# TensorE's order written out from the key projection to the last value product, in a Fourier and attention layer

## The chip, the cores and the metric

The kernel runs on one core of a Trainium2 chip. The metric is the device time of one execution in microseconds. Its engines are named as the profile names them: PE (TensorE, the matmuls), ACT (ScalarE), DVE (VectorE), POOL (GpSimd) and SP, which issues most of the DMA transfers.

## The reference

One layer of a generative model is computed for 128 context tokens and 1024 latent tokens, 1152 in all, with a width of 1024. Each layer is a normalisation with per-token-kind scale and shift, one joint projection, a Fourier mixer and a windowed attention side by side, a gated merge, and then an MLP.

```python
def merge_branches(u_f, attn_o, g, w_fo, w_ao, w_out):
    gates = jax.nn.sigmoid(g)
    g_f, g_a = gates[..., :D_MODEL], gates[..., D_MODEL:]
    m = g_f * (fourier_mix(u_f) @ w_fo) + g_a * (attn_o @ w_ao)
    return m @ w_out

def latent_layer(x, mod, k_ctx, v_ctx, cos, sin, g1, g2, w_in, sink, w_fo, w_ao, w_out, w_ff1, w_ff2):
    sh1, sc1, ga1, sh2, sc2, ga2 = mod
    h = rmsnorm(x, g1) * (1 + sc1) + sh1
    u_f, q, k, v, g = split_projection(h, w_in)
    ...
    attn_o = latent_attention(q, k, v, k_ctx, v_ctx, sink)
    x = x + ga1 * merge_branches(u_f, attn_o, g, w_fo, w_ao, w_out)
    h = rmsnorm(x, g2) * (1 + sc2) + sh2
    x = x + ga2 * channel_mixer(h, w_ff1, w_ff2)
    return x
```

The six vectors `sh1` to `ga2`, the modulation, are `silu(c) @ w_ada + b_ada`, with a weight of 1024 x 6144. Queries and keys are rotated (rotary embedding), and each block of 128 latent tokens sees three blocks of latent keys and 128 cached context keys. There are 16 query heads in four groups; a group shares one key and value head.

## The kernel before

All data is fp32. For a matmul an operand is split into a high and a low part in a shorter format: ACT casts the high part, DVE subtracts it to get the low one (`whi` and `wlo` for a weight, line 146 and line 141). One product is then three matmuls: high by high, high by low, low by high. The normalised input is held transposed in `BR` and `BT`, high and low.

The stages in the order of time are these (times of the profiled execution):

- 0 to 85 us: the normalisation, and the projection `u` of the Fourier branch.
- 85 to 182 us: the Fourier mix, four groups of channels. Products with cosine and sine matrices (`dhi`, `dlo`) alternate with casts of their results (`pqh`, line 555). Gate projections (tile `mm`, results `z` to the scratch tensor `z_d`) fill PE between them.
- 182 to 260 us: keys and values, `tok_proj_round`: round 0 for six tiles of 128 tokens, round 1 for three, in six PSUM banks. A round runs over eight slices k of the weight; in each k a tile gets three matmuls of 512 columns (lines 232 to 234), so 18 matmuls per k in round 0 and 9 in round 1. `evac_kv` splits the values, rotates the keys, stores both (`vh_d`, `kr_d`) and copies the keys of group 0 to `kd` (line 702, POOL). Then the queries of group 0, `q_pieces(0)`: six pieces of 24 matmuls with 384 columns, in two PSUM banks `mm`, rotated by DVE, stored to `q_d` and read back transposed as `qT` (line 736).
- 260 to 710 us: 36 attention units, one for each group and block of tokens. A unit has four score products (lines 755, 756), softmax, transposes of the probabilities (line 789) and value products (lines 804, 805) into one accumulator bank `o`, which `out_v` evacuates through `ot` and `at` (line 814) and stores to `att_d`. Pieces of later queries and gates stand as filler between these. For the first 34 units PE's order is the order of the code (a manual schedule); everywhere else a scheduler orders the instructions of each engine.
- 680 to 756 us: the last units, the projection of the Fourier result (`f_unit`, lines 910, 912 and 926: for each of eight blocks of 128 columns 13 matmuls of 512 columns and 13 of 130), results by ACT and DVE (`kd` and `macc`, later `fo` and `fy`, lines 914 to 917) to `part_d`; then the attention output is read back as `z` (line 1116) and split into `ER` (line 1128 and line 141).
- 756 to 980 us: the product with `w_ao`, the gated merge, the product with `w_out`. From 980 us the MLP.

The modulation vectors of the later parts are computed beside all this, without PE, in 16 blocks of ten steps (`mod_blocks`), each block 256 columns of `w_ada`. Steps 0 to 7 load 128 KB (`mraw`, line 305), let ACT scale it twice (line 309) into `macc` or, from step 1, into the only buffer `mprod`, and let POOL add it (line 311). Steps 8 and 9 are a transpose and a sum on DVE (lines 327, 328) into `red`. A fold, `mod_fold`, is one small matmul `mm <- red, quads` (line 274) with four DVE sums behind it; it is issued at step 5 of the following block. `mod_step(n)` issues n steps. Before the change 40 steps lie in the Fourier mix, 72 in the attention units, 8 behind them and 40 in the MLP. From the tail on the scalings and sums run on DVE alone (lines 316, 318).

Of the kernel before, what the change touches and what calls it, by code (L numbers as in the profile page):

```python
# [57 lines left out]
def backbone_kernel(  # L58
# [284 lines left out]
    with ExitStack() as sf:  # L343
# [175 lines left out]
        for gi in range(4):  # L519
# [71 lines left out]
            mod_step(MOD_F)  # L591

    with ExitStack() as s1x:
# [4 lines left out]
        identr = p1.tile([P, P], F32R, name="identr")  # L598
        nc.scalar.copy(identr, ident)
# [66 lines left out]

        with ExitStack() as skv:
# [59 lines left out]
            tok_proj_round(ROUNDS[0], OFF_KV, bankk, evac_kv)  # L727
            tok_proj_round(ROUNDS[1], OFF_KV, bankk, evac_kv)
# [67 lines left out]
        def out_v(u, b):  # L796
            k0, nb = KWIN[u["i"]]
            if b == 0:
                u["o"] = q1.tile([P, 512], F32, tag="o", name=nm("o"), bufs=1)
            po = u["o"]  # L800
            ph, pl = u["p"].pop(b)
            kb = {"c": 9, "x": 8}.get(KT_ORDER[k0 + b], KT_ORDER[k0 + b])
            vst = u["v"][:, kb].rearrange("p a d -> p (a d)")
            nc.tensor.matmul(po, vst, ph, start=(b == 0), stop=False)
            nc.tensor.matmul(po, vst, pl, start=False, stop=(b == nb - 1))
            if b < nb - 1:
                return
            ot = p1.tile([P, 2, P], F32, tag="ot", name=nm("ot"), bufs=1)
            at = p1.tile([P, 2, P], F32, tag="at", name=nm("at"), bufs=1)
            pv = po.rearrange("p (r e t) -> p e r t", r=2, e=2)  # L810
            for e in range(2):
                top, bot = slice(64 * e, 64 * e + 64), slice(64 - 64 * e, 128 - 64 * e)
                nc.scalar.copy(ot[top], pv[bot, e])
                nc.vector.tensor_tensor(at[top], pv[top, e], ot[top], ALU.add)
# [26 lines left out]

        fexw = (slot(8)[:, 0:FC][0:96], slot(9)[:, 0:D][0:96])

        def load_fx():
            wfo.append(load_wfo(0))
            for i in range(4):
                raw = raw_w([P, FC])
                nc.sync.dma_start(raw, f_d[i])
                hi, lo = (slot(2 * i + e)[:, 0:FC] for e in range(2))
                nc.scalar.copy(hi, raw)  # L850
                sub(nc.vector, lo, raw, hi)
                fx.append((hi, lo))
            raw = raw_w([P, FC])
            nc.gpsimd.memset(raw, 0.0)
# [10 lines left out]
            nc.scalar.copy(wex, raw[0:96])  # L865
            sub(nc.vector, wex[64:68], raw[64:68], wex[64:68])
# [17 lines left out]
        funits = [(m, j) for m in range(KC) for j in range(2)]  # L884
        fbank = [mmt]
        fbuf = []

        def f_mm(ps, ops, ex, c, r, n):
            wh, wl = wfo[0]
# [4 lines left out]
            if ex is not None:  # L894
                seq.append((ex, fexw[0]))
            for i, (w, x) in enumerate(seq):
                yield ps, w, x[:, r], i == 0, i == len(seq) - 1

        def f_unit(n):
            for _ in range(min(n, len(funits))):  # L900
                m, j = funits.pop(0)
                if m % 2 == 0 and j == 0 and m:
                    wfo[0] = load_wfo(m)
                c = slice((m % 2) * P, (m % 2) * P + P)
                wex = fexw[1][:, m * P : (m + 1) * P]
                if j == 0:
                    lat = slice(0, 512)
                    psy, psx = fbank[0](), fbank[0]()
                    for ps, w, x, a, z in f_mm(psy, (2, 3), None, c, lat, 512):
                        nc.tensor.matmul(ps, w, x, start=a, stop=z)  # L910
                    for ps, w, x, a, z in f_mm(psx, (0, 1), wex, c, lat, 512):
                        nc.tensor.matmul(ps, w, x, start=a, stop=z)
                    y, o = fbuf[0]()
                    nc.scalar.copy(y, psy)
                    nc.vector.tensor_tensor(o[:, 0:512], psx, y, ALU.subtract)
                    nc.vector.tensor_tensor(o[:, 1023:512:-1], psx[:, 1:512], y[:, 1:512], ALU.add)
                    nc.scalar.copy(o[:, 0:1], psx[:, 0:1])
                    nc.sync.dma_start(part_d[m][:, 0:512], o[:, 0:512])
                    nc.sync.dma_start(part_d[m][:, 513:1024], o[:, 513:1024])
                    continue  # L920
                ps = fbank[0]()
                ctx_ = list(f_mm(ps, (0, 1), wex, c, slice(512, 642), 130))
                cty_ = list(f_mm(ps, (2, 3), None, c, slice(512, 640), 128))
                for _, w, x, _, _ in ctx_[:1] + cty_ + ctx_[1:]:
                    n = x.shape[1]
                    nc.tensor.matmul(ps[:, 0:n], w, x, start=x is ctx_[0][2], stop=x is ctx_[-1][2])
                z = zpool[0].tile([P, CH], F32, tag="z", name=nm("z"), bufs=ZB[0])
                nc.scalar.copy(z[:, 0:130], ps[:, 0:130])
                nc.sync.dma_start(part_d[m][:, 1024:1152], z[:, 0:128])
                nc.sync.dma_start(part_d[m][:, 512:513], z[:, 128:129])  # L930

        def fbuf_p1():
            y = p1.tile([P, 2, MB], F32, tag="macc", name=nm("macc"), bufs=1)
            o = p1.tile([P, 10, 2, HD], F32, tag="kd", name=nm("kd"), bufs=1)
            return y.rearrange("p a n -> p (a n)"), o.rearrange("p a b d -> p (a b d)")

        fbuf.append(fbuf_p1)
# [3 lines left out]
        man = ExitStack()  # L941
        man.enter_context(tc.manual_schedule(engines={mybir.EngineType.PE}))
        for piece in q_pieces(0):
            for _ in piece:
                pass
        for q in range(3):
            put_k(kv[0][0], q)

        blocks_, pieces_ = [], []
        gate_left = gate_ids[48 - len(gates) :]  # L950
        share = -(-len(gate_left) // NG)
        gw = {}
        for g in range(NG):
            if g + 1 < NG:
                ws = q_weights(g + 1)
                for n, pc in enumerate(q_pieces(g + 1, ws)):
                    pieces_.append((pc, len(blocks_) + n % 2, g + 1 if n == 5 else None))
                blocks_ += ws
            for _ in range(min(share, len(gate_left))):
                m, j = gate_left.pop(0)  # L960
                if m not in gw:
                    gw[m] = (OFF_GF + m * P, {}), len(blocks_)
                    blocks_.append(gw[m][0])
                pieces_.append((gate_piece(m, j, gw[m][0]), gw[m][1], None))
        NSUB = KC * len(pieces_)
        qdone = {0}
        done = [0]

        def fill_steps():
            for pc, b, q in pieces_:  # L970
                for w in blocks_[: b + 2]:
                    fetch(w)
                for _ in pc:
                    yield
                if q is not None:
                    qdone.add(q)
                yield
# [13 lines left out]
        NMAN = len(units) - 2  # L991
# [3 lines left out]
        def begin(s):  # L995
            g, i = units[s]
            for g1, i1 in units[s : s + 4 : 3] if i % 3 == 0 else ():
                if (g1, i1 // 3) not in qts:
                    assert g1 in qdone, (s, g1)
# [3 lines left out]
        def next_keys(g, i):  # L1003
            if i == 0 and g:
# [25 lines left out]
        base, pending, late = 0.0, None, []  # L1030
        for s in range(NMAN):
            u = begin(s)
            order = unit_order(s, u, pending, late)
            share = NSUB * weight(s) / wsum
# [9 lines left out]
            pending = u  # L1044
        fill_to(NSUB)
        for _ in steps_:
            pass
        man.close()
        for s in range(NMAN, len(units)):
            u = begin(s)  # L1050
            for h in range(4):
                score_head(u, h)
                if late:
                    out_v(*late.pop(0))
            nb = KWIN[pending["i"]][1]
            for b in range(nb):
                out_t(pending, b)
                out_v(pending, b)
            pending = u
            if s == NMAN:  # L1060
                load_fx()
            f_unit(NF)
        mod_step(len(msteps) - MOD_B)
        mod_fold()
        f_unit(NF2)
        for b in range(KWIN[8][1]):
            out_t(pending, b)
            out_v(pending, b)
# [1022 lines left out]
```

## Time and profile before

| | us |
|---|---|
| runs | 1690.02, 1695.48, 1694.44 |
| median | 1694.44 |
| the profiled execution | 1695.82 |
| its span | 1694.0 |
| PE busy | 1624.9 (96%) |
| DVE busy | 1134.8 (67%) |
| ACT busy | 912.3 (54%) |
| POOL busy | 290.4 (17%) |

The span runs from the first to the last instruction of the profile; the 1.8 us beside it lie around the program. A busy time of 96% is a mean over the stages: it is near the whole in most of them and lower in the tail. A PE that is busy need not be at its full pace, since its clock is granted in parts; the mean clock over the span is 0.984 of full speed. In a view of waits, "PE o L804 <- DVE at L814: 10.5, 3, 4.1" reads: the matmul of line 804 into `o` waited three times for the DVE instruction of line 814 that writes `at`, 10.5 us in all and 4.1 us at the longest.

### The profile page before, as it was taken

The numbers are of one execution on the slowest core, as the hardware profiler recorded it, in microseconds if no ns is written. First come the engines' busy times: TensorE is split into PE (matmuls) and PEld (weight loads), VectorE is DVE, ScalarE is ACT, GpSimd is POOL, SyncE is SP. The second block draws the span as 40 slices with busy tenths as digits, with TensorE's granted clock in tenths as the row PEclk, the third lists the DMA queues.
The fourth block names the chain that finished last, engine by engine and source line by source line (L and its number), as shares of the span: only waits on it lengthen the run. The fifth ranks groups of instructions, "written<-read, shape, count | busy, mean of one in ns | idle before, by whom it ended". The sixth has DMA issues, their size and how long they took to land.

```text
span 1694.0 us, 24957 instructions
## 1 busy us (share of the span) xinstructions
PE 1624.9 (96%) x8421; PEld 1430.3 (84%) x8421; DVE 1134.8 (67%) x2147; ACT 912.3 (54%) x1775; POOL 290.4 (17%) x382
## 2 busy tenths in 40 slices
PE   6999998999999999789999899999999999999998
PEld 5789888899999999679988788888888888888886
DVE  7665266767767766657657876777776488776764
ACT  7766225676676766536436664444444353444542
POOL 1055013344344344500001500000000200000000
PEclk9999999999999999879999999999999999999999
DMA  8353487535453432468546434455446996666751
GB/s 300 125 171 105 164 212 162 130 102 131 122 137 101 130 95 77 135 192 290 162 172 202 153 109 149 163 168 168 159 152 156 307 389 196 194 195 191 248 162 63
DMA packets 221136, 285.41 MB, mean 168 GB/s; under 512 B 30968, under 2 KB 148664, under 8 KB 220880
## 3 DMA queue, kind: packets, MB, share of 16 engines
q1 hardware_dynamic: 212752, 273.85, 51.3%
q0 software_dynamic: 8256, 9.96, 2.6%
q8 instruction: 66, 1.08, 0.3%
q14 instruction: 62, 0.51, 0.1%
HBM read 205.87 MB, written 77.88 MB: 167 GB/s over the span
## 4 chain that ended last, share of the span: by engine, by line
PE 49%; DVE 2%; issue 2%; ACT 1%; DMA 1%; POOL 0%; SPq 0%; POOLq 0%; ACTq 0%; DVEq 0%
PE x L1817 6%; PE x L1816 6%; PE x L1818 6%; PE x L1420 6%; PE x L1422 6%; PE x L1421 6%; PE x L196 2%; PE x L194 2%; PE x L195 2%; PE mm L1467 1%; PE mm L1466 1%; PE mm L1465 1%; PE mm L1817 1%; PE mm L1816 1%; PE mm L1818 1%
## 5 line engine op out<-in xcount | busy, mean ns | idle before, releaser
L141 DVE TENSOR_TENSOR wlo<-wraw,whi 128x1024 fp32r<-128x1024 f32 x109 | 138.9, 1277 | 77.4 <-ACT whi L146 76.9
L146 ACT CAST whi<-wraw 128x1024 fp32r<-128x1024 f32 x107 | 111.8, 1049 | 91.5 <-PE x L1253 17.8
L767 ACT ACTIVATE pt<-pt,mx 128x513 f32<-128x513 f32 (+2 forms) x144 | 95.9, 666 | 78.5 <-DVE mx L757 73.5
L195 PE MATMUL mm<-BR,whi 128*128 128x384 f32 x408 | 138.0, 338 | 0.0
L779 POOL TENSOR_SCALAR pt<-pt,mx 128x512 f32<-128x512 f32 (+2 forms) x144 | 94.0, 665 | 237.1 <-DVE mx L777 230.3
L1817 PE MATMUL x<-BR 128*128 128x512 f32 (+1 forms) x348 | 132.9, 382 | 0.0
L1818 PE MATMUL x<-BR 128*128 128x512 f32 (+1 forms) x348 | 132.3, 382 | 0.0
L311 POOL TENSOR_TENSOR macc<-macc,mprod 128x512 f32<-128x512 f32 x84 | 113.5, 1352 | 108.3 <-ACT mprod L309 97.3
L194 PE MATMUL mm<-BR,whi 128*128 128x384 f32 x360 | 128.9, 358 | 2.7 <-DVE qt L638 1.9
L1816 PE MATMUL x<-BR 128*128 128x512 f32 (+1 forms) x348 | 131.4, 382 | 0.0
L757 DVE CUSTOM_DVE_ANT_0 pt<-s,mask,nsink 128x512 f32<-128x512 f32 (+2 forms) x144 | 96.1, 671 | 42.5 <-PE s L756 40.4
L196 PE MATMUL mm<-BR,wlo 128*128 128x384 f32 x360 | 122.1, 339 | 0.0
L1789 ACT CAST BR<-aa 128x512 fp32r<-128x512 f32 x80 | 49.7, 621 | 104.3 <-PE x L1817 46.4
L141 DVE TENSOR_TENSOR pl<-ptp,ph 128x512 fp32r<-128x512 f32 x124 | 83.0, 686 | 28.9 <-ACT ph L792 28.3
L309 ACT ACTIVATE mprod<-mraw,siluc 128x256 f32<-128x256 f32 x168 | 76.8, 505 | 32.1 <-POOL macc L311 31.8
L1420 PE MATMUL x<-BR,whi 128*128 128x512 f32 (+2 forms) x204 | 79.9, 391 | 4.1 <-ACT ZR L1444 2.8
L195 PEld LDWEIGHTS mm<-BR,whi 128*128 128x128 f32 x408 | 77.8, 191 | 6.3
L1421 PE MATMUL x<-BR,whi 128*128 128x512 f32 (+2 forms) x204 | 78.1, 383 | 0.0
L1422 PE MATMUL x<-BR,wlo 128*128 128x512 f32 (+2 forms) x204 | 78.0, 383 | 0.0
L792 ACT CAST ph<-ptp 128x512 fp32r<-128x512 f32 x124 | 69.9, 583 | 14.1 <-PE ptp L789 13.0
L194 PE MATMUL mm<-BT,whi 128*128 128x384 f32 x216 | 76.9, 356 | 0.0
L141 DVE TENSOR_TENSOR BR<-aa,BR 128x512 fp32r<-128x512 f32 x80 | 55.0, 687 | 32.2 <-ACT BR L1789 31.6
(448 smaller groups left out, 4750.7 us busy)
## 6 DMA issues: line engine op xcount, KB each, us to landing
aa<-hr_d SPq DMA_DIRECT2D x108, 256.0 KB
ab<-in_w_ff_dram SPq DMA_DIRECT2D x108, 256.0 KB
hr_d<-ZR SPq DMA_DIRECT2D x104, 256.0 KB
wraw<-in_w_in_dram SPq DMA_DIRECT2D x41, 512.0 KB
wraw<-in_w_ff_dram SPq DMA_DIRECT2D x34, 512.0 KB
mraw<-in_w_ada_dram SPq DMA_DIRECT2D x96, 128.0 KB
wraw<-in_w_out_dram SPq DMA_DIRECT2D x24, 512.0 KB
z_d<-z SPq DMA_DIRECT2D x48, 192.0 KB
```

Of the source, the lines that this page charges most:

```text
L141: eng.tensor_tensor(dst, raw, hi.bitcast(F32), ALU.subtract)
L146: nc.scalar.copy(hi, raw)
L194: nc.tensor.matmul(out, ah, bh, start=start, stop=False)
L195: nc.tensor.matmul(out, ah, bl, start=False, stop=False)
L196: return nc.tensor.matmul(out, al, bh, start=False, stop=stop).ins
L311: nc.gpsimd.tensor_tensor(acc, acc, pr_, ALU.add)
L1420: nc.tensor.matmul(po, wh, xh, start=(k == 0 and not cont), stop=False, skip_group_check=cont)
L1421: nc.tensor.matmul(po, wh, xl, start=False, stop=False, skip_group_check=cont)
L1422: nc.tensor.matmul(po, wl, xh, start=False, stop=(k == 3), skip_group_check=cont)
L1816: nc.tensor.matmul(ps, xh, bh, start=start, stop=False, skip_group_check=cont)
L1817: nc.tensor.matmul(ps, xh, bl, start=False, stop=False, skip_group_check=cont)
L1818: nc.tensor.matmul(ps, xl, bh, start=False, stop=stop, skip_group_check=cont)
```

## The change

The manual schedule of PE begins ahead of key round 0 and lasts to the last value product. Its order is now: round 0, the six query pieces of group 0, round 1, the first key transposes, twelve filler steps, the next key transposes, four filler steps, all 36 units.

The modulation steps leave the Fourier mix. Fifty stand in the key rounds, issued through `before=`: four for each k in round 0, two for each k in round 1 (four at the last). `tok_proj_round`, which itself is unchanged, issues those of two k ahead: with `ahead = 2` the steps of k = 0, 1 and 2 come before the matmuls of k = 0. The attention units keep 60, ten go to the ao product, 40 to the MLP.

The Fourier projection is written as pieces. Three (`FATT`) are filler in the last two units, five follow the last value product, in the six banks of the next stage. Two of its output buffers alternate, and the buffer `at` is doubled. The weight `wex` is spread over two slots, and the copy `identr` goes.

```diff
-MOD_B = 40
-MOD_F = 10
+MOD_B = 50
 MOD_LATE = 40
-NF = 4
-NF2 = 2
+FATT = 3
...
             filler(FILL_F, anchor)
-            mod_step(MOD_F)
...
-            tok_proj_round(ROUNDS[0], OFF_KV, bankk, evac_kv)
-            tok_proj_round(ROUNDS[1], OFF_KV, bankk, evac_kv)
+            man.enter_context(tc.manual_schedule(engines={mybir.EngineType.PE}))
+            tok_proj_round(ROUNDS[0], OFF_KV, bankk, evac_kv, before=lambda k: mod_step(4))
+            for piece in q_pieces(0):
+                for _ in piece:
+                    pass
+            tok_proj_round(ROUNDS[1], OFF_KV, bankk, evac_kv, before=lambda k: mod_step(2 if k < 7 else 4))
...
-            at = p1.tile([P, 2, P], F32, tag="at", name=nm("at"), bufs=1)
+            at = p1.tile([P, 2, P], F32, tag="at", name=nm("at"), bufs=2)
...
+        def f_piece(m):
+            if m % 2 == 0 and m + 2 < KC:
+                wfo.append(load_wfo(m + 2))
+            out = []
+            for ops, ex in (((2, 3), False), ((0, 1), True)):
+                ps = fbank[0]()
+                seq = f_mm(m, ops, ex)
+                for i, (w, x) in enumerate(seq):
+                    nc.tensor.matmul(ps, w, x[:, 0:512], start=i == 0, stop=i == len(seq) - 1)
+                    if i % 2 == 1 and i < len(seq) - 1:
+                        yield
+                out.append(ps)
...
+            nc.vector.tensor_tensor(o[:, 0:512], psx, y, ALU.subtract)
+            nc.vector.tensor_tensor(o[:, 1023:512:-1], psx[:, 1:512], y[:, 1:512], ALU.add)
...
-        NSUB = KC * len(pieces_)
+        NSUB = KC * len(pieces_) + FSUB * FATT
+        FX_AT = len(pieces_) - 2
...
+                if n == FX_AT:
+                    load_fx()
...
+            for _ in range(FATT):
+                for _ in f_piece(fleft.pop(0)):
+                    yield
+                yield
...
-        NMAN = len(units) - 2
+        NMAN = len(units)
...
+        put_k(kv[0][0], 0)
+        fill_to(12)
+        put_k(kv[0][0], 1)
+        fill_to(16)
...
+        for v in late:
+            out_v(*v)
+            fill_to(base + 1)
+        out_t(pending, 0)
         fill_to(NSUB)
         for _ in steps_:
             pass
+        out_v(pending, 0)
         man.close()
-        for s in range(NMAN, len(units)):
-            u = begin(s)
...
-            f_unit(NF)
         mod_step(len(msteps) - MOD_B)
         mod_fold()
-        f_unit(NF2)
```

PE at the start of round 0, before the change. The rows are the last gate filler of the Fourier mix, a fold whose steps lay in the Fourier mix, and then the first tile of round 0 (`x_1872`).

```order
L195 MATMUL mm_1744<-BR,whi_1712 128x384
L196 MATMUL mm_1744<-BT,wlo_1713 128x384
L274 MATMUL mm_1801<-red_1617,quads 128x16
L232 MATMUL x_1872<-whi_1868,BR 128x512
L233 MATMUL x_1872<-wlo_1869,BR 128x512
L234 MATMUL x_1872<-whi_1868,BR 128x512
```

PE after the change, at the end of k = 0 of round 0: the last tile of k = 0 (`x_1723`), the first fold, and the first tile of k = 1 (`x_1703`).

```order
L230 MATMUL x_1723<-whi_1699,BR 128x512
L231 MATMUL x_1723<-wlo_1700,BR 128x512
L232 MATMUL x_1723<-whi_1699,BR 128x512
L272 MATMUL mm_1745<-red_1679,quads 128x16
L230 MATMUL x_1703<-whi_1699,BR 128x512
L231 MATMUL x_1703<-wlo_1700,BR 128x512
L232 MATMUL x_1703<-whi_1699,BR 128x512
```

The fold that stood ahead of round 0 belonged to steps of the stage before; now the first block of the steps starts at round 0 and its fold stands behind 18 matmuls. The second stands behind 54 more, the third behind the query pieces, the fourth behind 36 matmuls of round 1.

ACT in the Fourier mix, before, around the first cast of `pqh`. The names are the scalings (`mprod`), the weight casts (`whi`) and the gate results (`z`).

```order
L309 ACTIVATE mprod_1380<-mraw_1378,siluc 128x256 x2
L146 CAST whi_1335<-wraw_1333 128x1024
L480 COPY z_1001<-mm_976 128x384
L309 ACTIVATE mprod_1386<-mraw_1384,siluc 128x256 x2
L146 CAST whi_1712<-wraw_1710 128x1024
L555 CAST pqh_1066<-x_1036 128x512
L309 ACTIVATE mprod_1392<-mraw_1390,siluc 128x256 x2
L555 CAST pqh_1066<-x_1037 128x256
```

ACT at the same place after the change:

```order
L478 COPY z_973<-mm_948 128x384
L144 CAST whi_1538<-wraw_1536 128x1024
L478 COPY z_1001<-mm_976 128x384
L553 CAST pqh_1066<-x_1036 128x512
L553 CAST pqh_1066<-x_1037 128x256
L531 CAST sth_1175<-st_1165 128x1152
```

The scalings are gone from between the casts; the weight cast stands one gate result earlier.

PE in the last unit after the change. The rows are a Fourier piece (`mm_7683`, line 926), scores of the last unit (`s`), and value products of the unit before it (`o_7666`). Before the change the Fourier products of lines 910 and 912 followed the scores of unit 34 in one run.

```order
L926 MATMUL mm_7683<-BR,whi_7335 128x512 x2
L755 MATMUL s_7689<-kth,qT_6925 128x128
L756 MATMUL s_7689<-ktl,qT_6925 128x128
L804 MATMUL o_7666<-ph_7641,vg_5606 128x512
L805 MATMUL o_7666<-pl_7642,vg_5606 128x512
L926 MATMUL mm_7683<-BR,wlo_7336 128x512
L926 MATMUL mm_7683<-BR,whi_7335 128x512
L755 MATMUL s_7698<-kth,qT_6925 128x128
L756 MATMUL s_7698<-ktl,qT_6925 128x128
L926 MATMUL mm_7683<-BR,whi_7335 128x512
```

Scores, value products and pieces alternate by ones and twos.

More of the change, by code (lines that the diff above doesn't have):

```diff
@@ L840, in backbone_kernel, with __getitem__ @@
         fx, wfo = [], []
-        fexw = (slot(8)[:, 0:FC][0:96], slot(9)[:, 0:D][0:96])
+        class Wex:
+            def __getitem__(self, idx):
+                o = idx[1].start
+                return slot(9 + o // 512)[:, o % 512 : o % 512 + idx[1].stop - o][0:96]
+        fexw = (slot(8)[:, 0:FC][0:96], Wex())
         def load_fx():
@@ L864, in load_fx @@
                 nc.sync.dma_start(raw[32 * k : 32 * k + 4], w_fo.rearrange("(g c) n -> g c n", g=4)[:, 64])
-            nc.scalar.copy(wex, raw[0:96])
-            sub(nc.vector, wex[64:68], raw[64:68], wex[64:68])
+            for o in range(0, D, 512):
+                r = slice(o, o + 512)
+                nc.scalar.copy(wex[:, r], raw[0:96, r])
+                sub(nc.vector, wex[:, r][64:68], raw[64:68, r], wex[:, r][64:68])
         def load_wfo(m):
@@ L882, in load_wfo, with fbuf_p1, f_mm @@
             return split(xy, [P, 4, 256])
-        funits = [(m, j) for m in range(KC) for j in range(2)]
         fbank = [mmt]
         fbuf = []
-        def f_mm(ps, ops, ex, c, r, n):
-            wh, wl = wfo[0]
+        fturn = [0]
+        def fbuf_p1():
+            fturn[0] += 1
+            if fturn[0] % 2:
+                y = p1.tile([P, 2, MB], F32, tag="macc", name=nm("macc"), bufs=1)
+                o = p1.tile([P, 10, 2, HD], F32, tag="kd", name=nm("kd"), bufs=1)
+                return y.rearrange("p a n -> p (a n)"), o.rearrange("p a b d -> p (a b d)")
+            y = p1.tile([P, 2, MB], F32, tag="mprod", name=nm("mprod"), bufs=1)
+            o = p1.tile([P, 2, 516], F32, tag="pt", name=nm("pt"), bufs=4)
+            return y.rearrange("p a n -> p (a n)"), o.rearrange("p a n -> p (a n)")
+        fbuf.append(fbuf_p1)
+        def f_mm(m, ops, ex):
+            wh, wl = wfo[m // 2]
+            c = slice((m % 2) * P, (m % 2) * P + P)
             seq = []
@@ L893, in f_mm @@
                 seq += [(wh[:, i, c], xh), (wh[:, i, c], xl), (wl[:, i, c], xh)]
-            if ex is not None:
-                seq.append((ex, fexw[0]))
-            for i, (w, x) in enumerate(seq):
-                yield ps, w, x[:, r], i == 0, i == len(seq) - 1
-        def f_unit(n):
[L900 to L937, printed above, removed]
+            if ex:
+                seq.append((fexw[1][:, m * P : (m + 1) * P], fexw[0]))
+            return seq
+        def f_piece(m):
[10 more added lines that the diff above has]
+                out.append(ps)
+                if not ex:
+                    y, o = fbuf[0]()
+                    nc.scalar.copy(y, ps)
+                    yield
+            psx = out[1]
+            nc.vector.tensor_tensor(o[:, 0:512], psx, y, ALU.subtract)
+            nc.vector.tensor_tensor(o[:, 1023:512:-1], psx[:, 1:512], y[:, 1:512], ALU.add)
+            nc.scalar.copy(o[:, 0:1], psx[:, 0:1])
+            nc.sync.dma_start(part_d[m][:, 0:512], o[:, 0:512])
+            nc.sync.dma_start(part_d[m][:, 513:1024], o[:, 513:1024])
+            yield
+            ps = fbank[0]()
+            ctx_ = [(w, x[:, 512:642]) for w, x in f_mm(m, (0, 1), True)]
+            cty_ = [(w, x[:, 512:640]) for w, x in f_mm(m, (2, 3), False)]
+            seq = ctx_[:1] + cty_ + ctx_[1:]
+            for i, (w, x) in enumerate(seq):
+                n = x.shape[1]
+                nc.tensor.matmul(ps[:, 0:n], w, x, start=i == 0, stop=i == len(seq) - 1)
+                if i % 5 == 4:
+                    yield
+            z = zpool[0].tile([P, CH], F32, tag="z", name=nm("z"), bufs=ZB[0])
+            nc.scalar.copy(z[:, 0:130], ps[:, 0:130])
+            nc.sync.dma_start(part_d[m][:, 1024:1152], z[:, 0:128])
+            nc.sync.dma_start(part_d[m][:, 512:513], z[:, 128:129])
@@ L939, in backbone_kernel @@
+        FSUB = 9
+        fleft = list(range(KC))
+        def f_unit(n):
+            for _ in range(min(n, len(fleft))):
+                for _ in f_piece(fleft.pop(0)):
+                    pass
         units = [(g, i) for g in range(NG) for i in range(NTT)]
         kv = {0: load_kv(0, kd0)}
[L941 to L947, printed above, removed]
+        for tag, n in (("s", 2), ("o", 1)):
+            for _ in range(n):
+                q1.tile([P, 512], F32, tag=tag, name=nm(tag), bufs=n)
@@ L949, in backbone_kernel, with add_gate @@
         blocks_, pieces_ = [], []
         gate_left = gate_ids[48 - len(gates) :]
+        gate_left[-4:] = gate_left[-3:] + gate_left[-4:-3]
         share = -(-len(gate_left) // NG)
         gw = {}
+        def add_gate():
+            m, j = gate_left.pop(0)
+            if m not in gw:
+                gw[m] = (OFF_GF + m * P, {}), len(blocks_)
+                blocks_.append(gw[m][0])
+            pieces_.append((gate_piece(m, j, gw[m][0]), gw[m][1], None))
         for g in range(NG):
+            if g == 0:
+                add_gate()
+                add_gate()
@@ L976, in fill_steps @@
                     qdone.add(q)
+                yield
+            for _ in range(FATT):
+                for _ in f_piece(fleft.pop(0)):
+                    yield
                 yield
@@ L1003, in next_keys @@
         def next_keys(g, i):
-            if i == 0 and g:
+            if i == 0:
                 put_k(kv[g][0], 2)
@@ L1028, in unit_order @@
             return out
-        base, pending, late = 0.0, None, []
+        put_k(kv[0][0], 0)
+        fill_to(12)
+        put_k(kv[0][0], 1)
+        fill_to(16)
+        base, pending, late = 16.0, None, []
+        NSPR = NSUB - 16 - 6
         for s in range(NMAN):
@@ L1033, in backbone_kernel @@
             order = unit_order(s, u, pending, late)
-            share = NSUB * weight(s) / wsum
+            share = NSPR * weight(s) / wsum
             spots, seen = order.count(None), 0
```

31 lines of the change are left out of this document (6 added, 25 removed).

## The prediction, made before the changed kernel ran

> **What bounds the kernel now.** I read the busy time by stage first, then what TensorE (PE) waited for, then the clock, and last the rows around each wait. Busy time of each engine in three stretches of the span: Fourier mix, key/value rounds, tail.
>
> ```profile
> 85.00:182.00 97.00, 92.88 (x504) 85.89 (x503) 54.33 (x96) 58.97 (x120) 45.78 (x36) 0.96 0.43 135
> 182.00:260.00 78.00, 76.03 (x376) 66.97 (x374) 33.51 (x65) 20.68 (x36) 6.42 (x16) 1.00 0.77 204
> 680.00:756.00 76.00, 57.04 (x278) 47.54 (x277) 42.36 (x89) 34.55 (x85) 20.22 (x28) 0.80 0.50 156
> ```
>
> The columns are stretch, length, busy us of PE, its weight loads, DVE, ACT and POOL, then the granted clock, the DMA share and GB/s. PE sets the end everywhere; the change leaves its work as it is, so the time can move only by PE's idle time and its slow clock. The tail stands out: 76.00 − 57.04 = 19.0 us idle, at a clock of 0.80. What PE waited for, over the span:
>
> ```profile
> PE o L804 <- DVE at L814: 10.5, 3, 4.1
> PE s L756 <- DVE ktl L141: 5.0, 1, 5.0
> PE x L910 <- DVE at L814: 3.8, 1, 3.8
> PE x L194 <- ACT pqh L555: 3.5, 1, 3.5
> PE mm L194 <- DVE qt L638: 1.9, 1, 1.9
> ```
>
> The first and third belong mostly to the tail. Seven stretches of the same view, cut by the granted clock (third figure from the right), show what such waits cost behind them:
>
> ```profile
> 127.95:134.70 6.75, 6.16 (x20) 5.08 (x19) 4.54 (x13) 2.29 (x6) 3.83 (x3) 0.50 0.21 68
> 241.00:243.00 2.00, 1.30 (x7) 1.31 (x8) 2.00 (x6) 1.09 (x3) 0.29 (x1) 1.00 1.08 359
> 264.50:271.20 6.70, 5.63 (x18) 5.63 (x19) 5.01 (x13) 3.19 (x7) 1.14 (x2) 0.50 1.22 277
> 701.40:715.00 13.60, 6.26 (x15) 4.10 (x14) 6.42 (x11) 6.34 (x14) 8.59 (x7) 0.50 0.39 112
> 728.70:735.50 6.80, 5.65 (x14) 4.47 (x14) 2.07 (x13) 0.58 (x1) 0.00 (x0) 0.50 0.45 125
> 739.00:745.60 6.60, 5.55 (x13) 3.87 (x13) 2.15 (x5) 1.69 (x5) 0.00 (x0) 0.50 0.90 273
> 752.60:755.80 3.20, 3.20 (x12) 3.20 (x11) 3.20 (x8) 2.26 (x6) 0.00 (x0) 0.50 0.98 319
> ```
>
> One more row of PE, the only wait at L804 that lies outside the tail:
>
> ```profile
> 310.31 0.48 PE L804 MATMUL o<-ph,vg 128*128 128x512 f32 x1 [2.86 <-DVE at L814]
> ```
>
> After waits of 3.5 and 5.0 us PE ran at half clock for 6.7 us; after the 1.9 us one it did not. Work done at half clock would have taken half its time. So the losses are: Fourier stage 3.5 + 6.16/2 = **6.6 us**; KV rounds and first units 1.9 + 5.0 + 5.63/2 + 2.9 = **12.6 us**; tail 19.0 + (6.26 + 5.65 + 5.55 + 3.20)/2 = **29.3 us**. These are all that the change can win.
>
> **The change, term by term.** The sum is made against the profiled execution, 1695.82 us (span 1694.0), 1.4 us over the median 1694.44 of the runs.
>
> *Fourier stage.* Forty modulation steps leave it. In the trace the cast `pqh` that PE waited for stood on ACT behind such a step, which waited for POOL, and behind a weight cast that waited for its load:
>
> ```profile
> 117.66 0.91 ACT L309 ACTIVATE mprod<-mraw,siluc 128x256 f32<-128x256 f32 x2 [0.74 <-POOL macc L311]
> 120.61 1.05 ACT L146 CAST whi<-wraw 128x1024 fp32r<-128x1024 f32 x1 [2.03 <-DMA wraw<-in_w_in_dram]
> 121.57 0.61 ACT L555 CAST pqh<-x 128x512 fp32r<-128x512 f32 x1
> ```
>
> Without the steps' scalings and loads it comes earlier. Bounds 2 to 6.6 us; I take **−6**, nearest to the whole since the wait and its half clock hang together.
>
> *KV rounds.* Fifty steps now stand here, and with PE's order written out, each block's fold (the small matmul `mm <- red`, L274 of before, L272 now) is a place at which PE stops until ACT, POOL and DVE have done the block's steps. The pace of a step, from seven POOL adds of one block (first and last):
>
> ```profile
> 156.40 1.29 POOL L311 TENSOR_TENSOR macc<-macc,mprod 128x512 f32<-128x512 f32 x1 [3.04 <-DVE pql L141]
> 171.00 1.30 POOL L311 TENSOR_TENSOR macc<-macc,mprod 128x512 f32<-128x512 f32 x1 [1.09 <-ACT mprod L309]
> 714.38 0.43 DVE L327 STREAM_TRANSPOSE mtr<-macc 128x256 f32<-128x256 f32 x1
> 715.78 0.42 DVE L328 TENSOR_REDUCE red<-mtr 128x8 f32<-128x256 f32 x1
> ```
>
> Six steps in 14.6 us are 2.4 us each, a chain through one `mprod` buffer: 0.9 (step 0) + 7 × 2.4 + 1.8 (four DVE instructions, 714.38 to 716.20) = 19.5 us for a block, and 18.3 for the next, whose first scalings go ahead. When it starts:
>
> ```profile
> 182.16 0.47 PE L232 MATMUL x<-whi,BR 128*128 128x512 f32 x1
> 185.49 0.33 SPq L601 DMA_DIRECT2D mask<-in_mask_dram  x1
> 188.90 2.06 SPq L305 DMA_DIRECT2D mraw<-in_w_ada_dram x3
> 196.55 0.91 ACT L309 ACTIVATE macc<-mraw,siluc 128x256 f32<-128x256 f32 x2 [0.32 <-DMA mraw<-in_w_ada_dram]
> ```
>
> The rounds began at 182.16; the weight loads stood behind mask, rotary tables and caches and ACT began at +14.4. The key rotary table and the caches are now loaded earlier, so I take +12 (from +6, about where the loads were issued, to +14). Queued behind a fold on PE are all later matmuls of the rounds, and behind the `mraw` loads on SP the later weight loads; ACT, POOL and DVE go on with the steps meanwhile. Fold 0 stands behind 18 matmuls and is ready at +31.5; fold 1 behind 72 matmuls and ready at 12 + 19.5 + 18.3 = +49.8. PE's own pace, from two rows 11 matmuls apart:
>
> ```profile
> 228.89 0.39 PE L234 MATMUL x<-whi,BT 128*128 128x512 f32 x1
> 231.39 0.39 PE L234 MATMUL x<-whi,BT 128*128 128x512 f32 x1
> ```
>
> 0.2275 us each: PE would be at fold 1 at 72 × 0.2275 = +16.4. So **33.4 us** are lost by then (27.4 to 35.4); the slow clock after fold 0 costs nothing beside it, since PE is early at fold 1 anyway. Folds 2 and 3 are covered: q(0)'s 144 matmuls (25 us) and half of round 1 lie between (a 384-column product at 384/512 of 0.2275 us).
>
> Behind fold 1: half clock again, 3 us by the row at 127.95. Then q(0)'s products need DVE, which has the six key tiles of round 0 to rotate first. In the trace ACT's first and last V casts of that round, and the read-back of q, stood at:
>
> ```profile
> 211.72 0.37 ACT L695 CAST qhl<-x 128x256 fp32r<-128x256 f32 x1 [3.71 <-PE x L234]
> 223.29 0.37 ACT L695 CAST qhl<-x 128x256 fp32r<-128x256 f32 x1 [4.70 <-DMA vh_d<-qhl]
> 245.64 1.85 SPq L736 DMA_DIRECT2D qT<-q_d  x4
> ```
>
> The six casts span 12 us, and DVE's rotations of their keys stand ahead of q's; the first two q pieces (48 matmuls, two banks) are only 8.2 us of PE: 0 to 8 us, I take 3. The q read-back is issued behind the last key store, 245.64 − 231.39 = 14 us after the rounds' last matmul; before, q's own matmuls covered that, now only key transposes and 48 gate matmuls, some 9 us, stand ahead of the first scores: 0 to 9 us, I take 5, the bare difference of the two. Sum 33.4 + 3 + 3 + 5 = 44.4, and the 12.6 of before go (`ktl`'s transposes come earlier, `at` has two buffers, the wait for q is counted anew): **+32** (+18 to +43).
>
> *Tail.* Three Fourier pieces now lie between the last scores and value products, the accumulator's evacuation has a second buffer, and five pieces follow on six banks. The waits for `at` go, with the half clock behind them. What is late next: the attention output's split (24 pairs, DVE) before the ao products, with ten modulation steps now among it.
>
> ```profile
> 752.17 3.44 DVE L141 TENSOR_TENSOR ER<-z,ER 128x384 fp32r<-128x384 f32 x7
> L318 DVE SCALAR_TENSOR_TENSOR ZR<-ZR,siluc 128x256 f32<-128x256 f32 x56 | 24.6, 476 | 1.1 <-DMA ZR<-in_w_ada_dram 1.0
> 755.53 0.68 DVE L915 TENSOR_TENSOR fo<-x,fy 128x512 f32<-128x512 f32 x1
> 726.20 0.27 PE L926 MATMUL mm<-BR,whi 128*128 128x130 f32 x1
> 726.31 0.27 PE L926 MATMUL mm<-BR,wlo 128*128 128x130 f32 x1
> ```
>
> 24 × 0.49 + 16 × 0.476 + 1.8 + 5 × 1.4 = 28 us on DVE (the splits, sixteen modulation products, their transposes, two `fo` sums for each of five pieces), against about 5 × (13 × 0.2275 + 13 × 0.11) = 22 us of PE's Fourier work (the 130-column products start 0.11 us apart): 3 to 8 us of wait, 1.7 to 3 of half clock, and 1 to 4 at the last values. About 10 us remain (5 to 16): **−19** (−13 to −24).
>
> The new second output buffer, the weights in two slots and the missing `identr` copy (0.3 us on ACT) hide behind PE and cost nothing; in the units PE's losses stay.
>
> Sum: −6 + 32 − 19 = **+7**: 1702.8, say 1702 us.
>
> **Rivals.**
>
> *The stall is shorter* (faster, 0.24). If the weight loads land as soon as they are issued (+6), nothing waits for q, and the tail runs with 5 us of loss, it is −7 + 18 − 24 = −13: 1683 us. For it: fewer loads queue ahead than before. Against: ACT's first scaling in the trace still waited for its load. It decides below a KV loss of about +20.
>
> *Balance* (within 0.3%, 0.22). Start at +9, half of the small waits: 30.4 + 3 + 3 + 2 − 12.6 = +26; with −6 and −19 this is +1: 1697 us.
>
> *The tail's clock stays low* (slower, 0.14). Two of its half-clock stretches began behind short waits:
>
> ```profile
> 728.12 0.62 PE L274 MATMUL mm<-red,quads 128*128 128x16 f32 x4 [0.64 <-ACT kd L917]
> 729.89 1.19 PE L910 MATMUL mm<-BR,whi 128*128 128x512 f32 x2 [1.15 <-DVE mods L278]
> 738.72 1.10 PE L910 MATMUL x<-BR,whi 128*128 128x512 f32 x2 [1.63 <-ACT fy L914]
> ```
>
> So 1.2 to 1.6 us among small matmuls were enough, and five pieces still follow one another over a few banks. Keeping the last three stretches costs (5.65 + 5.55 + 3.20)/2 = 7.2 us of the gain: 1709, at most 1710 us. [...]
>
> *All the new waits at their upper ends* (slower, 0.06): 35.4 + 3 + 8 + 9 − 12.6 = +43, with −6 and −19: 1714 us.
>
> That the folds do not bind would be the change not doing what it says; the order of PE's instructions shows them ahead of the matmuls, so it has no chance of its own.
>
> **How the numbers follow.** The forecast, 1702 (own range 1699.5 to 1707), has 0.34. A measurement of this kernel can tell about 0.3% (5 us) from no change. Faster by more: 0.24; within: 0.22; slower by more: 0.34 + 0.14 + 0.06 = 0.54. Signs differ, so the range runs from 1684 to 1717.
>
> **What would show it.** In the profile after: PE idle some 27 us before the first fold and 3 to 6 us before the second, released by DVE `red`, at half clock between; no wait for `pqh`; the tail's idle time halved, with no wait for `at` between the last units and the Fourier pieces, and a wait for the split of `z` before the ao products. I am wrong if the folds wait less than 25 us in all, or if the tail keeps over 20 us of loss.

## The result: 1720.7 us, slower by 1.6%

| | before | after |
|---|---|---|
| median of the runs, us | 1694.96 (4 runs) | 1720.71 (4 runs, 1719.39 to 1725.81) |
| ratio after to before, 95% interval | | 1.0163 [1.0133, 1.0192] |
| span of the profiled execution, us | 1694.0 | 1717.6 |

The change costs 26 us by the medians and 23.6 us by the two profiled spans. One of the five executions of e9 below took 5721.68 us; its ratio is taken from the other four. Busy time by stage in the profile after, in the columns of the prediction's first fence: Fourier mix, key rounds up to the first scores, attention units, tail up to the ao products.

```profile
85.00:174.00 89.00, 88.55 (x496) 82.37 (x496) 40.38 (x73) 33.91 (x58) 8.36 (x8) 1.00 0.35 110
174.00:318.00 144.00, 95.49 (x443) 84.02 (x442) 56.32 (x112) 61.40 (x123) 53.09 (x51) 0.82 0.61 154
318.00:700.00 382.00, 371.69 (x2155) 346.42 (x2155) 263.85 (x644) 256.19 (x596) 154.88 (x240) 1.00 0.41 115
700.00:785.00 85.00, 78.89 (x454) 70.09 (x454) 64.25 (x136) 48.19 (x114) 19.08 (x35) 0.98 0.59 181
```

PE's idle time is 0.5, 48.5, 10.3 and 6.1 us. To these belong the stretches at half clock, from the same view:

```profile
205.50:211.90 6.40, 6.36 (x16) 5.11 (x17) 0.63 (x4) 2.29 (x6) 3.63 (x3) 0.50 0.25 67
222.30:229.00 6.70, 4.37 (x14) 3.50 (x15) 2.78 (x8) 2.96 (x8) 2.56 (x2) 0.75 0.47 139
300.00:307.50 7.50, 4.92 (x17) 4.95 (x18) 1.12 (x2) 2.04 (x5) 2.60 (x4) 0.50 0.65 199
427.00:430.40 3.40, 3.40 (x13) 3.01 (x12) 1.03 (x3) 1.32 (x3) 1.13 (x2) 0.51 0.43 91
751.40:754.70 3.30, 3.30 (x10) 2.55 (x9) 0.00 (x0) 0.83 (x2) 0.00 (x0) 0.50 0.55 144
```

Half of the busy time there is counted as lost, as in the prediction: 3.2, 1.7 (the half clock is the second half of that stretch), 2.5, 1.7 and 1.7 us. That is a little much: at half clock products of 512 columns started 0.43 us apart (206.99 to 211.25 us), at full clock 0.2275 us, so 47% is lost by the rows. By stage, loss (idle time and half clock) before and after, in us:

| stage | before | after | difference | predicted |
|---|---|---|---|---|
| Fourier mix | 6.6 | 0.5 | −6 | −6 |
| key rounds to first units | 12.6 | 55.9 | +43 | +32 |
| attention units | 3.7 | 12.0 | +8 | 0 |
| tail | 29.3 | 7.8 | −21.5 | −19 |
| sum | | | +23.5 | +7 |

What PE waited for in the profile after:

```profile
PE mm L272 <- DVE red L326: 30.1, 2, 26.8
PE ptp L835 <- ACT rb L711: 16.4, 1, 16.4
PE o L804 <- DVE at L814: 9.2, 6, 2.3
...
PE x L926 <- DVE at L814: 2.2, 1, 2.2
...
PE x L192 <- ACT pqh L553: 0.4, 1, 0.4
```

The first row is the two folds, 26.8 and 3.3 us. The second is far above the 5 us that the prediction had ahead of the first scores: one wait of 16.4 us in front of the first key transposes, for the instruction that copies the context tile's values out (`rb`). Three rows of PE show all three, with the idle time at the end:

```profile
205.54 0.61 PE L272 MATMUL mm<-red,quads 128*128 128x16 f32 x2 [26.85 <-DVE red L326]
224.63 0.37 PE L272 MATMUL mm<-red,quads 128*128 128x16 f32 x2 [3.29 <-DVE red L326]
302.58 1.09 PE L835 MATMUL ptp<-ident,kd 128*128 128x128 f32 x4 [16.38 <-ACT rb L711]
```

`rb` and the transposes share no data: `rb` reads the bank of the last key tile, and the transposes write a bank of the next PSUM pool (`q1`), which lies on the same six banks. Of `kd` the transposes need tiles 0 to 2 and the cache alone. The profile puts the wait of their weight load down to the last copy into `kd`, which ended 0.1 us ahead of `rb`; e1 below tells the two apart. Why `rb` was so late, on ACT and on SP's queue:

```profile
289.52 1.04 ACT L144 CAST whi<-wraw 128x1024 fp32r<-128x1024 f32 x1 [7.57 <-DMA wraw<-in_w_in_dram]
...
291.74 0.35 ACT L691 CAST qhl<-x 128x256 fp32r<-128x256 f32 x1
...
297.14 1.04 ACT L144 CAST whi<-wraw 128x1024 fp32r<-128x1024 f32 x1 [3.77 <-DMA wraw<-in_w_in_dram]
300.08 0.37 ACT L691 CAST qhl<-x 128x256 fp32r<-128x256 f32 x1 [1.90 <-DMA vh_d<-qhl]
...
302.11 0.37 ACT L711 COPY rb<-x 128x256 f32<-128x256 f32 x1
```

```profile
282.50 0.91 SPq L153 DMA_DIRECT2D wraw<-in_w_in_dram  x1
283.50 8.70 SPq L303 DMA_DIRECT2D mraw<-in_w_ada_dram  x2
292.30 0.38 SPq L153 DMA_DIRECT2D wraw<-in_w_in_dram  x1
...
305.82 0.34 SPq L736 DMA_DIRECT2D qT<-q_d  x1
```

Round 1's last matmul began at 285.8. The first cast of its evacuation, `qhl`, stood on ACT behind a weight cast that waited 7.6 us for its load. The next load stood on SP behind `mraw` loads, which took 8.7 us to get out, and held up a second weight cast. The third `qhl` then waited another 1.9 us, for the store of the first to free its buffer, so that store ended last. The read-back of q, `qT`, followed at 305.8.

### The profile page after: what moved, and what is told of

Same layout as the page of the kernel before. It is cut to its first block, busy times and chain, and to the rows that moved or that the text cites. A ratio compares the mean times of both kernels' runs of the same rounds, so it can differ in the third digit from the quotient of the medians.

```text
span 1717.6 us, 24946 instructions
## 1 busy us (share of the span) xinstructions
PE 1621.3 (94%) x8421; PEld 1426.9 (83%) x8421; DVE 1133.9 (66%) x2164; ACT 909.4 (53%) x1759; POOL 279.1 (16%) x375
## 4 chain that ended last, share of the span: by engine, by line
PE 70%; DVE 5%; DMA 3%; ACT 3%; issue 2%; POOL 1%; SPq 1%; DVEq 0%; ACTq 0%; POOLq 0%
PE x L1845 6%; PE x L1843 6%; PE x L1844 6%; PE x L1447 6%; PE x L1449 6%; PE x L1448 6%; PE mm L192 4%; PE mm L194 4%; PE mm L193 4%; PE ptp L789 2%; PE x L194 2%; PE x L193 2%; PE x L192 2%; PE s L756 2%; PE o L805 2%
## 5 line engine op out<-in xcount | busy, mean ns | idle before, releaser
L309 POOL TENSOR_TENSOR macc<-macc,mprod 128x512 f32<-128x512 f32 x77 | 102.1, 1326 | 42.9 <-ACT mprod L307 32.8
L307 ACT ACTIVATE mprod<-mraw,siluc 128x256 f32<-128x256 f32 x154 | 70.2, 502 | 46.8 <-POOL macc L309 45.8
L1844 PEld LDWEIGHTS x<-BR 128*128 128x128 f32 x348 | 65.4, 188 | 12.9
```

The lines of the kernel that those rows point to most:

```text
L309: nc.gpsimd.tensor_tensor(acc, acc, pr_, ALU.add)
L1844: nc.tensor.matmul(ps, xh, bl, start=False, stop=False, skip_group_check=cont)
```

## The experiments

Each run has its median and its ratio to the kernel before, taken on the same chip. Theory A: the place of the folds in PE's written order costs. Theory B, its rival: the steps' load on the other engines does. Theories C and D concern the 16.4 us, E and F the tail.

**e1_folds_held.** The folds wait until the first units:

```diff
+    hold = [False]
+    spare = []
...
-        while fold:
+        while fold and not hold[0]:
...
+            hold[0] = True
             tok_proj_round(ROUNDS[0], OFF_KV, bankk, evac_kv, before=lambda k: mod_step(4))
...
+            hold[0] = False
```

> The changed kernel with its fifty modulation steps where they are, but the five folds held back until the first attention units (their sums kept in spare tiles). Theory A (it is the place of the folds in PE's written order that costs): the 30.1 us of waiting at L272 and the half clock behind them, 37 us in all by the profile, go; five folds in a row cost some 3 us; 1684 to 1690 us. Theory B (it is the steps' load on ACT, POOL and DVE that costs, wherever the folds stand): the wait only moves to the weight casts and to q's and the keys' evacuation; 1705 us or more.

1696.2 us, ratio 1.0004 [0.9992, 1.0016]: 24.5 us less than the changed kernel, between the two. Round 1's last matmul began at 252.8 instead of 285.8, 33 us earlier, as theory A has it, and the first scores at 278.0 instead of 315.3. Behind them some 13 us came back: among these, the five folds in a row cost 4.8 us of waits and left PE at half clock from 305.1 to 312.0. In front of the first scores two waits remain, for `rb` and for `qT`; the middle row is a wait in the rounds:

```profile
PE ptp L844 <- ACT rb L716: 9.9, 1, 9.9
...
PE mm L192 <- DVE qt L638: 3.5, 2, 3.2
PE s L764 <- DMA qT<-q_d: 3.5, 1, 3.5
```

The longest wait for q's evacuation is 3.2 us, where the changed kernel had one of 1.0 us in the rounds. Theory A carries 33 us; theory B is wrong for the rounds. Three rows show which wait the transposes have:

```profile
262.56 0.37 ACT L716 COPY rb<-x 128x256 f32<-128x256 f32 x1
263.03 1.09 PE L844 MATMUL ptp<-ident,kd 128*128 128x128 f32 x4 [9.87 <-ACT rb L716]
263.31 0.29 POOL L703 COPY kd<-qr 128x128 f32<-128x128 f32 x1
```

The transposes began 0.1 us behind the end of `rb` and ahead of the last copy into `kd`: they wait for the bank's reader, not for `kd`.

**e2_steps_back.** The steps return to the Fourier mix:

```diff
             filler(FILL_F, anchor)
+            mod_step(10)
...
-            tok_proj_round(ROUNDS[0], OFF_KV, bankk, evac_kv, before=lambda k: mod_step(4))
+            tok_proj_round(ROUNDS[0], OFF_KV, bankk, evac_kv)
...
-            tok_proj_round(ROUNDS[1], OFF_KV, bankk, evac_kv, before=lambda k: mod_step(2 if k < 7 else 4))
+            tok_proj_round(ROUNDS[1], OFF_KV, bankk, evac_kv)
```

> The changed kernel with no modulation steps in the key rounds and ten behind each group of the Fourier mix, as before the change. Theory A and theory B both: 37 us of fold waits and half clock go, 7 us of the Fourier mix (the wait for pqh) come back. Theory C (the 16.4 us in front of the first key transposes are the evacuation of round 1 with nothing ahead of it, made longer by steps and their loads): that wait falls to 10 to 12 us but stays; 1683 to 1690 us. If the wait were made by the steps alone, it would go: about 1674 us.

1683.3 us, ratio 0.9942 [0.9922, 0.9961], in the range: faster than before. Its waits:

```profile
PE ptp L836 <- ACT rb L712: 5.6, 1, 5.6
PE x L192 <- ACT pqh L553: 3.3, 1, 3.3
```

The wait for `pqh` is back with the steps, as the prediction's Fourier term has it. The wait for `rb` does not go, but at 5.6 us it is half of what was expected. Round 1's first `qhl` now begins 0.9 us ahead of the round's last matmul; in the changed kernel it began 5.9 us behind it.

**e3_gates_first.** The sixteen fillers first:

```diff
+        fill_to(16)
         put_k(kv[0][0], 0)
-        fill_to(12)
         put_k(kv[0][0], 1)
-        fill_to(16)
```

> The changed kernel with all sixteen filler steps ahead of the first key transposes instead of twelve between and four behind them: the same matmuls in another order. Theory C (the transposes' banks come free only when round 1 is evacuated, and 8.4 us of matmuls that need none of these banks stand behind them): the wait falls from 16.4 to about 8 us, 1710 to 1714 us. If the gate matmuls, too, wait for that evacuation: 1718 us or more.

1721.9 us, ratio 1.0158 [1.0139, 1.0177]: no gain, though the wait fell to 5.7 us. PE's rows:

```profile
302.88 0.45 PE L835 MATMUL ptp<-ident,kd 128*128 128x128 f32 x1 [5.73 <-ACT rb L711]
...
316.69 0.66 PE L755 MATMUL s<-kth,qT 128*128 128x384 f32 x1 [11.87 <-DMA qT<-q_d]
```

The first scores come at 316.7 as against 315.3. They wait for the read-back of q, which SP issues from 305.9 on and which lands some 10 us later. So theory C is half right: the fillers do cover the wait for the banks, but behind it runs a longer path, from round 1's last matmul through the evacuation, its last store and q's read-back to the first scores. It took 29.5 us with the steps in the changed kernel and 28.3 in e3, 25 in e1 and 20 in e2; the order of the sixteen fillers moves only where PE waits for it.

**e6_round0_only.** Round 1 is called without `before`, so that its eighteen steps fall to the units and six behind them.

> The changed kernel without the eighteen steps in round 1 (six of them then stand at the end of the units, the others within them). Theory D (the evacuation of round 1 is late since ACT stands in a weight cast that waits for its load, and the load stood on SP behind mraw loads without a free buffer): the wait at the first key transposes falls from 16.4 to about 10 us and the first two fold waits stay; 1712 to 1716 us. If the steps have no part in it: 1719 us or more.

1727.4 us, ratio 1.019 [1.017, 1.0211]: slower. The path became shorter, 21.5 instead of 29.5 us: the waits at its end are 5.5 and 4.4 us, and the first scores come at 306.6, 8.7 us earlier than in the changed kernel. So the steps of round 1 made it longer; whether by their loads on SP, as theory D has it, or by their work on ACT, the run does not tell. The loss is in the tail:

```profile
PE mm L947 <- ACT macc L932: 11.7, 1, 11.7
...
PE ptp L835 <- ACT rb L711: 5.5, 1, 5.5
PE s L755 <- issue: 4.4, 1, 4.4
```

The Fourier pieces put their results into `macc` and `mprod`, the steps' own buffers. With steps in the last units the two are in each other's way, and PE waited 11.7 us.

**b3_back_gates32.** e2 with 32 fillers ahead of the first transposes (`fill_to(32)`).

> The changed kernel with the steps back in the Fourier mix and, in addition, 32 filler steps (16.7 us of gate and query matmuls) ahead of the first key transposes instead of 12 and 4 around them. Theory C, as the last runs leave it: from the last matmul of round 1 a path of some 20 us (evacuation, read-back of q) leads to the first scores, and matmuls that need neither the key banks nor q cover it. The waits of 5.6 and 2.1 us there and the half clock behind them (3.4 us) go: 1673 to 1677 us, against 1683 without. If the fillers wait for their own two banks and for ACT, which evacuates the keys: 1681 us or more.

1682.4 us, ratio 0.9928 [0.9913, 0.9943]: like e2. The wait for the banks is gone, one of 3.7 us for `qT` is left, with no half clock behind it. Most of what that won was lost again in the units and the tail, where sixteen fillers are missing; that these are the reason was not tried.

**e7_at_one** gives `at` one buffer again (`bufs=1`); **e8_no_f_filler** sets `FATT = 0`. Both are the changed kernel otherwise.

> The changed kernel with one buffer for `at`, as before the change. If the second buffer carries the gain of the tail: the waits for `at` grow there by 4 us and more with a half clock behind them, 1726 to 1731 us. If the Fourier pieces between the products carry it: within 3 us of 1721 us.

> The changed kernel with no Fourier piece as filler: all eight follow the last value product. If the pieces between scores and value products carry the gain of the tail: the last units wait again, 10 to 15 us with the half clock, 1731 to 1736 us. If the second buffer of `at` and the steps' absence from the tail carry it: within 4 us of 1721 us.

1721.3 us, ratio 1.0159 [1.0142, 1.0176], and 1721.5 us, 1.0164 [1.0145, 1.0183]. Neither changes the time: neither part of the change by itself carries the gain of the tail. From 640 to 785 us alone e8 is not neutral: PE is idle there for 9.6 us at a clock of 0.96, against 8.4 us at 0.99 in the changed kernel, and makes that up ahead of it. What is left is that the last six units have no modulation steps, or PE's written order there.

**e9_before_stop.** The kernel before, with one number altered:

```diff
-MOD_B = 40
+MOD_B = 60
```

> The kernel before the change with one number altered: the units stop taking modulation steps at sixty left instead of forty, so that the last six units have none and none stand behind them (twenty go to the ao product). Theory E (the tail's gain comes from the steps' absence: with steps, ACT and POOL delay the evacuation of the last value products): the tail's loss falls from 29 to 10 to 14 us, 1675 to 1681 us. Theory F (it comes from PE's written-out order in the last two units): the tail's loss stays near 25 us, 1690 us or more.

1670.4 us, ratio 0.9848 [0.9829, 0.9867]: 26 us faster than before, and more than theory E asked for. The first row is its last units and tail, the second the stretch that the prediction shows of the kernel before:

```profile
640.00:730.00 90.00, 86.69 (x509) 78.31 (x508) 61.02 (x127) 52.43 (x120) 21.83 (x40) 1.00 0.45 144
680.00:756.00 76.00, 72.34 (x419) 66.05 (x418) 55.57 (x111) 43.01 (x96) 9.17 (x18) 1.00 0.76 243
```

From 680 to 756 us PE is idle for 3.7 us at full clock, where the kernel before was idle for 19.0 us at 0.80. How the steps stood in the way, rows of the kernel before show:

```profile
689.53 0.91 ACT L309 ACTIVATE macc<-mraw,siluc 128x256 f32<-128x256 f32 x2
705.45 0.77 PE L804 MATMUL o<-ph,vg 128*128 128x512 f32 x1 [3.52 <-DVE at L814]
710.46 1.19 PE L910 MATMUL x<-BR,whi 128*128 128x512 f32 x2 [3.82 <-DVE at L814]
715.30 0.45 DVE L327 STREAM_TRANSPOSE mtr<-macc 128x256 f32<-128x256 f32 x1
715.83 0.59 ACT L914 COPY macc<-mm 128x512 f32<-128x512 f32 x1 [2.75 <-DVE mtr L327]
```

and the same copies in e9:

```profile
691.57 0.59 ACT L914 COPY macc<-mm 128x512 f32<-128x512 f32 x1 [0.96 <-PE mm L910]
698.34 0.59 ACT L914 COPY macc<-mm 128x512 f32<-128x512 f32 x1 [1.12 <-PE mm L910]
705.95 0.59 ACT L914 COPY macc<-mm 128x512 f32<-128x512 f32 x1 [1.80 <-PE mm L910]
```

The Fourier projection copies its results into `macc`, the one buffer in which a block of steps is summed. The block that begins in the last unit and ends with the eight steps behind it held `macc` from 689.5 to 715.8 us. The Fourier products that PE finished at 694.5 thus kept both `mm` banks, no further ones could start there, and PE had only value products, which wait for their one accumulator. In e9 `macc` is free. The scheduler, whose order PE follows here in both kernels, then has 58 Fourier matmuls among the last value products (688.5 to 705.7 us), against 13 before (690.1 to 705.5 us). Before the change the Fourier products did not follow the scores of unit 34 in one run: from 673 to 694 us they stood in pieces among scores and value products, and the run of 91 came at 710.5, behind the last of these. The evacuation of an accumulator is hardly shorter: the last three take 3.0 to 4.6 us from the first copy `ot` to the end of the last sum `at`, against 3.3 to 4.8 us before. So theory E is right that the steps' absence carries the gain, but not by the evacuation that it names. A second buffer for the Fourier results, with the steps left in place, was not tried.

**e10_steps_in_tail.** e6 and e8 together: steps in all units, no Fourier piece between.

> The changed kernel without Fourier filler (as e8) and without the eighteen steps of round 1 (as e6), so that all units have two steps and six stand behind them, and no Fourier piece lies between. Theory E: the tail loses 20 us or more, against some 14 in e8; with the 8 us that e6 gained ahead of the first scores, 1720 to 1726 us. Theory F: the tail loses as in e8, 1712 to 1715 us.

1723.1 us, ratio 1.0165 [1.0144, 1.0185], as theory E expected. The first scores came at 305.7, 10.5 us earlier than in e8, and the first ao product at 776.8, like e8's 777.5: the 10 us were lost again. Some 6 of them went from unit 32 on, whose first scores came at 672.8 and, in e8, at 679.3; the others went earlier, in units that have two steps each in both runs. So steps in the last units cost time with PE's order written out as well, and theory F does not hold as it stands.

**b5_units_all** (b3 with no steps in the Fourier mix and `MOD_A = (2, 2)`) and **b7_fill40** (b5 with 40 fillers ahead).

> The kernel of b3_back_gates32 with no modulation steps in the Fourier mix either: the attention units take four each instead of two, until fifty are left, which is after unit 28. Theory: where PE waits for no fold and has fillers, the steps cost nothing; the 7 us of the Fourier mix go as well, 1666 to 1670 us. If the units' softmax on ACT, POOL and DVE becomes late by four steps a unit: 1676 us or more.

> The kernel of b5_units_all with 40 instead of 32 filler steps ahead of the first key transposes, 20.9 us against a path of 21 us. If more cover still gains, the wait of 4.4 us at the first score and the half clock behind it go: 1672 to 1675 us. If the fillers are then missing in the units: 1677 us or more.

1678.9 us, ratio 0.9906 [0.989, 0.9923], and 1679.7 us, 0.9907 [0.989, 0.9923]. The interval of b5 overlaps that of b3, so little is left of the Fourier mix's 7 us. With four steps in a unit, a wait of 6.0 us for `pl` appears in the units of b5, and the waits for `at` are 12.0 us in all, the tail included (9.2 in the changed kernel). More fillers ahead gain nothing more.

**b8_before_units.** e9 with `MOD_F = 0` and `MOD_A = (2, 2)`.

> The kernel before the change, with sixty steps left behind the units (as e9) and, besides, none in the Fourier mix: the units take four steps each, a hundred in the first 25 units. The 7 us of the Fourier mix go as well, of which b5 kept half against b3: 1663 to 1668 us. If the units become late by four steps each: 1671 us or more.

1672.3 us, ratio 0.9877 [0.9859, 0.9896], like e9. The Fourier mix and the units, in the view by stage:

```profile
85.00:182.00 97.00, 96.40 (x532) 88.96 (x531) 41.59 (x74) 35.23 (x61) 8.65 (x9) 1.00 0.36 116
320.00:640.00 320.00, 309.17 (x1779) 286.69 (x1778) 219.17 (x539) 227.81 (x536) 156.56 (x218) 0.98 0.45 120
```

The Fourier mix loses nothing, but the units are idle for 10.8 us at a clock of 0.98, against 3.5 us in e9: the steps took there what they gave here. e9 and b8 are the best versions found, and e9 is the kernel before with one number altered.

## Why the prediction was wrong

The prediction gave 1702 us and 1684 to 1717; the time is 1720.7. The sign was right, the sum too small by 17 us (1702.8 against the 1719.4 of the profiled execution). None of the signs of being wrong that it names came: the folds waited over 25 us and the tail kept under 20.

- **Fourier mix, −6: right.** The wait for `pqh` fell to 0.4 us. e2 brings the steps and the wait back.
- **Folds, 33.4 us and 3 us of half clock behind: right.** Measured: waits of 26.85 and 3.29 us, predicted 27 and 3 to 6, and 4.9 us of half clock; ACT's first scaling stood at +12.0, as taken. e1 shows that the place of the folds does it.
- **q's evacuation, 3 us: 1.0 us.**
- **The first scores, 5 us: this step failed.** The prediction said that "now only key transposes and 48 gate matmuls, some 9 us, stand ahead of the first scores: 0 to 9 us, I take 5, the bare difference of the two". Measured are 16.4 us before the transposes, 1.0 us before the scores and 2.5 us of half clock, 20 us. Two things were overlooked. The transposes are no cover: they are the first to write into the pool that takes over the key rounds' banks, and so wait for the last reader of round 1. And the path does not end with the issue of the read-back, which came 20 us behind round 1 instead of 14: it lands some 10 us later (e3). From round 1's last matmul to the first scores it is 20 us without steps (e2) and 29.5 with them, against 9 us of matmuls. Before the change q's own matmuls covered it; the change put them in front of round 1, and put steps beside it that made it longer.
- **Units, 0: failed, 8 us.** Small waits for `at` (1.1 to 2.3 us) and one half clock. e1 and e2 have them too, so the steps of the key rounds are not the cause. Fillers that are spread thinner, over 36 units and with sixteen spent ahead, would fit; it was not tried, and the cause stays open.
- **Tail, −19: the size was nearly right (−21.5), the reason incomplete, and the agreement in part luck.** The prediction put the gain down to the second buffer of `at`, the pieces between the products and the six banks, and did not name the steps that leave the last units. Without the second buffer (e7) or the pieces (e8) the time stays the same. e9 has neither the second buffer nor the written order and gains the whole: without steps `macc` is free, and Fourier products lie between the value products in the scheduler's order too. Of the waits expected to remain, the one for the split of `z` was 1.2 us instead of 3 to 8, and one of 2.2 us for `at`, which was to go, stayed. What each part of the change does beside that stays open.
- **Rivals.** The tail's clock did not stay low (0.98 in its row). A shorter stall and a balance went the other way, with smaller losses in the rounds than the 56 us measured. The upper ends of the new waits, 1714 us, came nearest, and still had the loss ahead of the first scores at 9 instead of 20 us.

## What to carry to other kernels

When work is moved ahead, look at what it covered where it stood: here q's matmuls hid an evacuation, a store and a read-back of 20 us, which no wait of the profile before shows. Here the first instruction of a new pool on old banks waited for the last reader of these banks, whatever its own data (16.4, 9.9 and 5.6 us in three of the runs), so it covered nothing. Two streams of work that shared a buffer stopped each other here: `macc`, held by a block of background steps for 26 us, kept PE from its filler. And in a change of several parts, try the smallest one by itself: the earlier stop of the modulation steps alone, 1670 us, gave more than any version with the written-out order that was tried (1679 us at best).

## What the runs showed of the hardware

Half clock followed some waits that are shorter than the 3.5 and 5.0 us of the prediction's first rows. Two of PE's rows in the profile after:

```profile
426.66 0.48 PE L804 MATMUL o<-ph,vg 128*128 128x512 f32 x1 [2.15 <-DVE at L814]
...
749.99 0.47 PE L926 MATMUL x<-BR,whi 128*128 128x512 f32 x1 [2.18 <-DVE at L814]
```

PE went to half clock for 3.3 to 3.4 us within 1.5 us of the end of each, while a wait of 2.29 us at 644 in the same run and the one of 2.86 us at 310 before the change were followed by none. Of the two short waits in the prediction's last fence only the one of 1.63 us ended ahead of its half clock, which began at 738.9; the half clock at 728.7 began with the wait of 1.15 us, 0.5 us behind the end of the one of 0.64 us. Other half-clock stretches lasted 3.2 to 3.4 us (from 752.6 before the change, from 225.6 after it), 6.6 to 6.9 us (from 127.95, 264.5, 728.7 and 739.0 before, from 305.1 in e1) and 13.6 us (from 701.4 before); two began within the long waits of the run after, at 181.3 and 290.6, and went on for 6.5 and 5.0 us behind them. What sets these lengths, and why of two waits of like length one was followed by half clock and the other not, no run here shows.
